# Other distances between the side steps of a Hyena filter, in a layer kernel that runs on one TensorE queue

## The chip, the cores and the metric

The kernel runs on one core of a Trainium2 chip, in one launch. The metric is device time in microseconds (us), the median of several runs. A profile of one execution shows what each engine did: TensorE (PE, with its weight loads as PEld), VectorE (DVE), ScalarE (ACT), GpSimd (POOL) and SyncE (SP). Each engine has one queue and works through it in order.

## The reference

One encoder layer in float32, 512 tokens of width 2048. A Hyena branch and an attention branch read the same normalised input, are gated and merged, and a SwiGLU network follows. The change concerns the Hyena branch, whose long filter comes out of a small network:

```python
def implicit_filter(L, w1, b1, w2, b2, w3, b3, w4, freq):
    ...
    h = jnp.sin(fr * (z @ w1 + b1))
    h = jnp.sin(fr * (h @ w2 + b2))
    h = jnp.sin(fr * (h @ w3 + b3))
    h = h @ w4
    ...
    h_fwd = h[:, :HYENA_W] * decay
    h_bwd = h[:, HYENA_W:] * decay
    k = jnp.concatenate([h_fwd, zeros, h_bwd[:0:-1]], axis=0)
    return k / jnp.sum(jnp.abs(k), axis=0, keepdims=True)

def bidir_fft_conv(u, k):
    uf = jnp.fft.rfft(u, n=2 * L, axis=1)
    kf = jnp.fft.rfft(k, n=2 * L, axis=0)
    return jnp.fft.irfft(uf * kf[None], n=2 * L, axis=1)[:, :L]

def hybrid_layer(...):
    proj = rms_norm(x, mix_norm_g) @ w_in
    u_h, q, k, v, g = jnp.split(proj, [c0, c1, c2, c3], axis=-1)
    x0, x1, hv = jnp.split(centred_short_conv(u_h, hy_conv_w, hy_conv_b), 3, axis=-1)
    z = hv * x1
    y_h = (bidir_fft_conv(z, filt) + hy_bias * z) * x0
    ...
```

## The kernel before

Activations lie transposed: 128 channels on the partitions, 512 tokens along the row. Weights come in 128x128 blocks, eight to a tile (`wr`), through SP's queue. ScalarE rounds a tile to a high part (`wh`), VectorE subtracts to get the low part (`wl`), with three buffers for each (`wblk`, L175). A **product** is the three matmuls (high x high, high x low, low x high) of one weight block with one row block of x (`mm3`, L199).

TensorE's matmuls stand in the order in which the program is written. The main stream is: 64 products for the first four column blocks of `w_in` (x1 and hv of the first two channel blocks, `px`), 16 for each further column (`px`, `phv`; three columns to a channel block, eight channel blocks in four quarters), so 384 products in all; then 64 steps for the keys and values (`kv`, products 384 to 448), then the queries (`q`). Each finished Hyena column gets a short convolution (L576): one multiplication by the row scale `rbc` and two scalar forms on VectorE, one activation on ScalarE. x1 and hv of a channel block give `z`, and `zf`, its two halves.

Between the products stand **side steps**. They are Python generators in one queue. After each product the function `step()` (L144) lowers a counter, and when it is at zero it runs the front generator up to its next `yield n`, which sets the counter to n products. The numbers behind `yield` are therefore distances on TensorE, in products. For each quarter q the side steps are, in order:

- `mlp_gen` (L312, once): the three layers of the filter network (`hp` on TensorE, then seven operations on VectorE and a sine on ScalarE), MLP_WAIT products apart
- `taps_gen`: four pairs of tap matmuls (`fp`), two products apart; VectorE multiplies them with the decay (`fd`, `bd`) and folds them into a sum and a difference (`hs`, `hd`)
- `filter_gen`: transposes of these (`ktp`), a turn and a split on ScalarE and VectorE (`kr`, `k000h`, `k000l` and the like), the halved transform (`kp`), from it the spectra `G` and `K`, which go to DRAM (`kd`, POOL's queue)
- `conv_gen`: transposes of z (`ztp`, split into `zt`), the forward transform (`up`), the product with the filter's spectrum, read back from DRAM (`kc`), on VectorE (`cu`, `cv`, `Y`, split into `Yt`), the taps of the next quarter, and the inverse transform (`ab`), whose result times x0 is `yh`.

PSUM has eight banks for all of this. After the kv chunk, `flush()` runs what is left of the queue, the pool of the Hyena buffers is given up, and the rope table `rpk` is loaded by ScalarE's queue into memory that they held. Keys are normalised and rotated (`vh`, `kscr`, `kqn`, `ko`) and transposed (`kT0p`) 20 products into the queries.

The lines that the change touches: MLP_WAIT (L36), W_FETCH (L55) with the branch of it in `wblk` (L190 to 194), and the distances in `filter_gen` and `conv_gen`.

Of the kernel before, what the change touches and what calls it, by code (L numbers as in the profile page):

```python
# [11 lines left out]
F32 = mybir.dt.float32  # L12
F32R = mybir.dt.float32r
AF = mybir.ActivationFunctionType
ALU = mybir.AluOpType
# [8 lines left out]
NQ = 4  # L24
# [8 lines left out]
HYENA_LAST = 0, 13, 14, 15  # L33
ATT_LAST = 4, 5, 6, 7, 0, 1, 2, 3
G_EARLY = 7
MLP_WAIT = 26  # L36
Z_WAIT0 = 16
N_WARM = 10
XW = 4
# [12 lines left out]
STD_ORDER = (*range(EARLY_ACTS, NSTD), *range(EARLY_ACTS))  # L52
NEARLY = 5
W_FIRST = 16, 72
W_FETCH = ()  # L55

C_X0, C_X1, C_HV, C_Q, C_KV, C_GH, C_GA = 0, 1024, 2048, 3072, 4096, 4608, 6656

# [57 lines left out]
def layer_kernel(tc, wpk, xT, par, flt, zemb, w4, decT, tb2, rope, qkg, out):  # L116
    nc = tc.nc
# [12 lines left out]
    def ps_tile(name):  # L130
        return banks["pool"].tile([P, S], F32, tag="ps", bufs=banks["n"], name=name)
# [4 lines left out]
    def transpose(out, src):  # L136
        tc.keep_in_program_order(nc.tensor.transpose(out, src, ident))
# [31 lines left out]
    def tmp(name):  # L169
        return tpool.tile([P, S], F32, tag="tmp", bufs=5, name=name)  # L170
# [4 lines left out]
    def wblk(nb=1):  # L175
        st = state
        if st["pos"] >= BLK:
            i = st["tile"]
            raw = wpool.tile([P, BLK * P], F32, tag="raw", bufs=2, name=f"wr{i}")
            hi = wpool.tile([P, BLK * P], F32R, tag="whi", bufs=3, name=f"wh{i}")  # L180
            lo = wpool.tile([P, BLK * P], F32R, tag="wlo", bufs=3, name=f"wl{i}")
            st.update(tile=i + 1, pos=0, hi=hi, lo=lo, raw=raw)

        i, n = st["tile"] - 1, {1: XW // 2, 2: XW}.get(st["tile"], BLK)
        if st["pos"] % n == 0:
            c = slice(st["pos"] * P, (st["pos"] + n) * P)
            with tc.high_priority() if W_FIRST[0] <= i < W_FIRST[1] else nullcontext():
                nc.sync.dma_start(st["raw"][:, c], wpk[i, :, c])
                nc.scalar.copy(st["hi"][:, c], st["raw"][:, c])  # L189
                if i in W_FETCH:  # L190
                    nc.scalar.activation(st["lo"][:, c], st["raw"][:, c], AF.Copy, scale=-1.0)
                    nc.gpsimd.dma_start(st["lo"][:, c], wpk[i, :, c], accum_op=ALU.add)
                else:
                    nc.vector.tensor_tensor(st["lo"][:, c], st["raw"][:, c], st["hi"][:, c].bitcast(F32), ALU.subtract)  # L194
        a = st["pos"] * P
        st["pos"] += nb
        return st["hi"][:, a:a + nb * P], st["lo"][:, a:a + nb * P]

    def mm3(ps, ah, al, bh, bl, first, last, **kw):  # L199
        mm(ps, ah, bh, first, False, **kw)  # L200
        mm(ps, ah, bl, False, False, **kw)
        mm(ps, al, bh, False, last, **kw)

    def group(ps, act, k0=0, k1=None):
        n = len(act)
        for k in range(k0, n if k1 is None else k1):
            wh, wl = wblk()
            mm3(ps, wh, wl, act[k][0], act[k][1], k == 0, k == n - 1)
            step()

    def split(pool, src, th, tl, bh, bl, name):
        hi = pool.tile([P, S], F32R, tag=th, bufs=bh, name=name + "h")
        lo = pool.tile([P, S], F32R, tag=tl, bufs=bl, name=name + "l")
        nc.scalar.copy(hi, src)
        nc.vector.tensor_tensor(lo, src, hi.bitcast(F32), ALU.subtract)
        return hi, lo
# [27 lines left out]
    def pcol(name, i=0):  # L244
        a = PC[name] + i
        return prm[:, a:a + 1]
# [45 lines left out]
    def work(name):  # L292
        return cw(name, [P, S], "wk", 7)
# [7 lines left out]
    def part(i, low, a, b):  # L301
        return CS[i][:, low * S + a:low * S + b]
# [9 lines left out]
    def mlp_gen():  # L312


        hcur = zem
        yield MLP_WAIT
        w4_load(0)
        for l in range(3):
# [14 lines left out]
            if l == 2:  # L333
# [4 lines left out]
                mlp["h"] = hh, hl  # L338
            yield MLP_WAIT
            if l == 0:  # L340
# [5 lines left out]
    def w4_load(q):  # L346
        w4t[q] = tmp(f"w4r{q}")
        for h in range(2):
            nc.scalar.dma_start(w4t[q][h * 64:(h + 1) * 64], w4[q])

    def w4_parts(q):

        w4r = w4t[q]
        w4h = tpool.tile([P, S], F32R, tag="tmp", bufs=5, name=f"w4h{q}")
        w4s = cw(f"w4s{q}", [P, 512], "w4s", 1, F32R)
        nc.scalar.copy(w4h[64:], w4r[64:])
        nc.scalar.copy(w4s[:64], w4r[:64])
        nc.vector.tensor_tensor(w4s[64:], w4r[64:], w4h[64:].bitcast(F32), ALU.subtract)
        w4t[q] = w4s
# [40 lines left out]
    def filter_gen(q):  # L400
        rn, hs_l, hd_l = folded.pop(q)
        if q + 1 < NQ:
            w4_load(q + 1)
        taps = []
        for i, src in enumerate((hs_l, hd_l)):
            tps = [ps_tile(f"ktp{q}{i}{j}") for j in range(2)]
            for j, tp in enumerate(tps):
                for n in range(4):
                    o = n // 2 * 256 + j * P
                    transpose(tp[:, n * P:(n + 1) * P], src[n % 2][:, o:o + P])  # L410
            for j in range(2):
                t = tmp(f"kt{q}{i}{j}")
                nc.scalar.activation(t, tps[1 - j], AF.Copy, scale=pcol("sina" if i == j else "nsina"))
                turned = work(f"kr{q}{i}{j}")
                nc.vector.scalar_tensor_tensor(turned, tps[j], pcol("cosa"), t, ALU.mult, ALU.add)
                taps.append(split(cv, turned, "kh", "kl", 4, 4, f"k{i}{q}{j}"))
            yield 3
        if q + 1 < NQ:
            w4_parts(q + 1)
        yield 6  # L420


        kd[q] = dpool.tile([256, 6 * 256], F32, tag=f"kd{q}", bufs=1, name=f"kd{q}")
        spectra = [], []
        for i in range(2):
            g = [ps_tile(f"kp{q}{i}{w}") for w in range(2)]
            for w in range(2):
                mm3(g[w], part(w, 0, 3 * P, 4 * P), part(w, 1, 3 * P, 4 * P), *taps[2 * i + (w ^ i)], True, True)
            cc = tmp(f"kc{q}{i}")
            nc.scalar.copy(cc, g[0])  # L430
            for fb, (a, b, op) in enumerate(((g[1], cc, ALU.add), (cc, g[1], ALU.subtract))):
                spectra[fb].append(work(f"G{q}{fb}{i}"))
                nc.vector.scalar_tensor_tensor(spectra[fb][i], a, pcol("inner"), b, ALU.mult, op)
            yield 3
        for fb in range(2):
            g = spectra[fb]
            sin, nsin = ("sinw", "nsinw")[::1 - 2 * fb]
            cr, ci = tmp(f"kcr{q}{fb}"), tmp(f"kci{q}{fb}")
            nc.scalar.activation(cr, g[0], AF.Copy, scale=pcol("cosw", fb))
            nc.scalar.activation(ci, g[1], AF.Copy, scale=pcol("ncosw" if fb else "cosw"))  # L440
            k1, k2, k3 = (work(f"K{i}{q}{fb}") for i in range(3))
            nc.vector.scalar_tensor_tensor(k1, g[1], pcol(sin, fb), cr, ALU.mult, ALU.add)
            nc.vector.scalar_tensor_tensor(k2, g[0], pcol("nsinw", fb), ci, ALU.mult, ALU.add)
            nc.vector.scalar_tensor_tensor(k3[:, :256], g[1][:, 256:], pcol(nsin, fb), cr[:, 256:], ALU.mult, ALU.add)
            nc.vector.scalar_tensor_tensor(k3[:, 256:], g[0][:, 256:], pcol("sinw", fb), ci[:, 256:], ALU.mult, ALU.add)
            rows = kd[q].rearrange("(p s) c -> p s c", s=2)[:, 1 - fb]
            nc.gpsimd.dma_start(rows[:, :S], k3)
            for i, k in enumerate((k1, k2)):
                nc.gpsimd.dma_start(rows[:, S:].rearrange("p (a b c) -> p a b c", a=2, b=2)[:, :, i],
                                    k.rearrange("p (a c) -> p a c", a=2))  # L450
        filt[q] = rn

    zst, x0st, yh = {}, {}, [None] * HT

    def conv_gen(q):
# [37 lines left out]
                yield 5  # L493
        if q + 1 < NQ:
            yield from taps_gen(q + 1)
        yield 8 if q + 1 < NQ else 14
        abs_ = [work(f"abs{2 * q + c}") for c in range(2)]
        for ph in range(2):
            ab = [ps_tile(f"ab{q}{ph}{c}") for c in range(2)]
# [34 lines left out]
    queue(taps_gen(0))  # L534
    queue(pause(12))
    queue(filter_gen(0))
    w00 = wblk()
    for k in range(KT):
        xr = r3.tile([P, S], F32, tag="r", bufs=16, name=f"xr{k}")
        nc.sync.dma_start(xr, xT[k])  # L540
        hl = r1[k < HT].tile([P, 2 * S], F32R, tag="hl", bufs=HT, name=f"xh{k}")
        hi, lo = hl[:, :S], hl[:, S:]
# [42 lines left out]
    for q in range(NQ):  # L585
        zl, zf_l = [], []
        for c in range(2):
# [19 lines left out]
            zf_l.append(zf)  # L607
        zst[q] = (zl, zf_l, side["n"] + (Z_WAIT0 if q == 0 else 10))
        queue(conv_gen(q))
        if q + 1 < NQ:  # L610
            queue(filter_gen(q + 1))
# [866 lines left out]
```

## Time and profile before

| | us |
|---|---|
| median of 3 runs (2528.24 to 2529.08) | 2528.87 |
| the profiled execution, as a whole | 2527.96 |
| its span in the profile | 2526.2 |
| mean granted TensorE clock in it | 0.999 of full speed |
| end of the last inverse transform of the Hyena branch | 377.2 |

Times in the profile count from the start of the span. A line of a timeline gives start, duration, engine, source line, operation, output and inputs, and in brackets the idle time before it and what ended that. A line of the waits gives the waiting engine and line, whom it waited for, and in us the total, the number of waits and the longest. A line of the windows gives, for a stretch of time, its length and the busy time of each engine with its number of instructions, then the granted clock and the DMA share and rate.

### The profile page before, as it was taken

What the parts mean: (1) busy time and instruction counts of PE and PEld (TensorE: products, weight loads), DVE (VectorE), ACT (ScalarE), POOL (GpSimd) and SP (SyncE); (2) the same over time, 40 slices, a digit from 0 to 9 for tenths busy, and PEclk for the clock granted to TensorE, in tenths of its full rate; (3) what the DMA queues carried; (4) which work ended last, traced back from release to release, by engine and by line L of the source; (5) the groups of instructions that cost most, each with busy time, mean ns of one, the idle gap of its engine ahead of it and who ended that gap; (6) DMA issues with size and microseconds to landing.
All of it is one profiled execution on the core that took longest, in us unless ns stands there. A gap on an engine that the chain in (4) does not pass through costs nothing.

```text
span 2526.2 us, 34432 instructions
## 1 busy us (share of the span) xinstructions
PE 2499.9 (99%) x13114; PEld 2143.5 (85%) x13114; DVE 2089.0 (83%) x2968; ACT 1194.9 (47%) x1779; POOL 182.8 (7%) x295
## 2 busy tenths in 40 slices
PE   9999999999999999999999999999999999999999
PEld 7777778888888888888888888888888888888888
DVE  7889884766479999754899899989998988998888
ACT  6533433655355455443544444444444445445443
POOL 0001112110000000000000000000000002001111
PEclk9999999999999999999999999999999999999999
DMA  6334443222554444544333333333333349557754
GB/s 213 109 116 140 130 131 113 84 80 101 175 175 162 155 139 158 191 164 145 119 112 125 117 120 131 109 134 113 130 121 121 118 137 223 149 146 184 193 156 109
DMA packets 113538, 350.42 MB, mean 139 GB/s; under 512 B 13987, under 2 KB 15267, under 8 KB 113148
## 3 DMA queue, kind: packets, MB, share of 16 engines
q1 hardware_dynamic: 70128, 248.02, 29.6%
q0 software_dynamic: 22832, 63.19, 9.6%
q10 hardware_dynamic: 20412, 37.00, 4.7%
q8 instruction: 103, 1.69, 0.3%
q14 instruction: 63, 0.52, 0.1%
HBM read 297.56 MB, written 54.26 MB: 139 GB/s over the span
## 4 chain that ended last, share of the span: by engine, by line
PE 79%; DVE 1%; ACT 0%; issue 0%; ACTq 0%
PE fx L134 19%; PE fy L134 10%; PE b L134 7%; PE o L134 7%; PE gx L134 6%; PE d L134 5%; PE fz L134 5%; PE dx L134 4%; PE ex L134 3%; PE gy L134 3%; PE ey L134 2%; PE dy L134 2%; PE gz L134 2%; PE q L134 1%; PE dz L134 1%; PE av L134 1%
## 5 line engine op out<-in xcount | busy, mean ns | idle before, releaser
L194 DVE TENSOR_TENSOR wl<-wr,wh 128x1024 fp32r<-128x1024 f32 (+1 forms) x168 | 201.2, 1198 | 123.2 <-ACT wh L189 122.9
L189 ACT CAST wh<-wr 128x1024 fp32r<-128x1024 f32 (+1 forms) x168 | 173.2, 1031 | 274.2 <-PE o L134 66.0
L901 ACT CAST fwhs<-fs 128x1024 fp32r<-128x1024 f32 x176 | 184.9, 1051 | 87.5 <-PE fz L134 69.1
L903 DVE TENSOR_TENSOR fwls<-fs,fwhs 128x1024 fp32r<-128x1024 f32 x176 | 214.3, 1218 | 4.5 <-ACT fwhs L901 4.4
L901 ACT CAST fwha<-fa 128x1024 fp32r<-128x1024 f32 x132 | 139.0, 1054 | 151.1 <-PE fx L134 82.9
L134 PE MATMUL px<-xh,wh 128*128 128x512 f32 x576 | 180.9, 396 | 0.0
L134 PE MATMUL fx<-fX,fwhs 128*128 128x512 f32 x704 | 175.4, 391 | 0.6 <-DVE fv L945 0.6
L134 PE MATMUL fy<-fX,fwhs 128*128 128x512 f32 x704 | 175.5, 391 | 0.0
L134 PE MATMUL fx<-fX,fwha 128*128 128x512 f32 x704 | 172.0, 391 | 0.2 <-DVE c L950 0.2
L903 DVE TENSOR_TENSOR fwla<-fa,fwha 128x1024 fp32r<-128x1024 f32 x132 | 161.3, 1222 | 9.9 <-ACT fwha L901 9.7
L134 PE MATMUL o<-ms,wh 128*128 128x512 f32 x512 | 157.7, 389 | 0.0
L134 PEld LDWEIGHTS fx<-fX,fwhs 128*128 128x128 f32 x704 | 129.3, 188 | 25.7 <-DVE fv L945 0.9
L134 PEld LDWEIGHTS fx<-fX,fwha 128*128 128x128 f32 x704 | 129.3, 188 | 25.4 <-issue 0.6
L134 PEld LDWEIGHTS fy<-fX,fwhs 128*128 128x128 f32 x704 | 129.4, 188 | 24.8
L134 PEld LDWEIGHTS px<-xh,wh 128*128 128x128 f32 x576 | 107.5, 189 | 24.7 <-issue 2.4
L134 PE MATMUL d<-act,wh 128*128 128x512 f32 x384 | 118.3, 390 | 0.0
L134 PE MATMUL px<-xh,wl 128*128 128x512 f32 x288 | 113.1, 393 | 0.0
L134 PEld LDWEIGHTS o<-ms,wh 128*128 128x128 f32 x512 | 96.1, 188 | 19.9
L894 DVE TENSOR_TENSOR fs<-fa,fa 128x1024 f32<-128x1024 f32 x88 | 107.1, 1217 | 1.7 <-PE o L134 1.0
L894 DVE TENSOR_TENSOR fs<-fs,fa 128x1024 f32<-128x1024 f32 x88 | 107.3, 1219 | 1.0 <-PE o L134 0.2
L134 PE MATMUL o<-ms,wl 128*128 128x512 f32 x256 | 99.7, 389 | 0.0
L134 PE MATMUL fy<-fX,fwls 128*128 128x256 f32 x704 | 98.7, 283 | 0.0
(970 smaller groups left out, 5909.0 us busy)
## 6 DMA issues: line engine op xcount, KB each, us to landing
fa<-wpk SPq DMA_DIRECT2D x176, 512.0 KB, 3.9
wr<-wpk SPq DMA_DIRECT2D x162, 512.0 KB, 3.5
ga<-wpk SPq DMA_DIRECT2D x60, 512.0 KB, 3.9
da<-wpk SPq DMA_DIRECT2D x32, 512.0 KB, 3.8
ea<-wpk SPq DMA_DIRECT2D x32, 512.0 KB, 4.2
actd<-c POOLq DMA_DIRECT2D x41, 256.0 KB, 4.3
actr<-actd ACTq DMA_DIRECT2D x41, 256.0 KB, 4.2
x2d<-dt POOLq DMA_DIRECT2D x32, 256.0 KB, 5.4
```

Of the source, the lines that this page charges most:

```text
L134: tc.keep_in_program_order(nc.tensor.matmul(out, lhsT=lhsT, rhs=rhs, start=start, stop=stop, **kw))
L189: nc.scalar.copy(st["hi"][:, c], st["raw"][:, c])
L194: nc.vector.tensor_tensor(st["lo"][:, c], st["raw"][:, c], st["hi"][:, c].bitcast(F32), ALU.subtract)
L894: raws["sum"] = nc.vector.tensor_tensor(t, a, b, ALU.add).ins
L901: nc.scalar.copy(hi, w)
L903: raws["wl"] = nc.vector.tensor_tensor(lo, w, hi.bitcast(F32), ALU.subtract).ins
```

## The change

The layers of the filter network come 20 products apart in place of 26. In each quarter twelve products more are put around side steps: two ahead of the transposes of the filter (`ktp`), three ahead of the halved transform (`kp`), two behind its last part, and three (in the last quarter two) ahead of the inverse transform (`ab`). With what the queue itself takes for a generator's end, the distance from the last `kp` to `ztp` goes from four products to eight. A branch that was never taken is removed.

```diff
-MLP_WAIT = 26
+MLP_WAIT = 20
...
-W_FETCH = ()
...
-                if i in W_FETCH:
-                    nc.scalar.activation(st["lo"][:, c], st["raw"][:, c], AF.Copy, scale=-1.0)
-                    nc.gpsimd.dma_start(st["lo"][:, c], wpk[i, :, c], accum_op=ALU.add)
-                else:
-                    nc.vector.tensor_tensor(st["lo"][:, c], st["raw"][:, c], st["hi"][:, c].bitcast(F32), ALU.subtract)
+                nc.vector.tensor_tensor(st["lo"][:, c], st["raw"][:, c], st["hi"][:, c].bitcast(F32), ALU.subtract)
...
     def filter_gen(q):
         rn, hs_l, hd_l = folded.pop(q)
         if q + 1 < NQ:
             w4_load(q + 1)
+        yield 2
         taps = []
...
         if q + 1 < NQ:
             w4_parts(q + 1)
-        yield 6
-
+        yield 9
...
             for i, k in enumerate((k1, k2)):
                 nc.gpsimd.dma_start(rows[:, S:].rearrange("p (a b c) -> p a b c", a=2, b=2)[:, :, i],
                                     k.rearrange("p (a c) -> p a c", a=2))
+            yield 2
         filt[q] = rn
...
         if q + 1 < NQ:
             yield from taps_gen(q + 1)
-        yield 8 if q + 1 < NQ else 14
+        yield 11 if q + 1 < NQ else 16
```

Counted on TensorE's queue, the steps stand behind these products:

| step | quarter 0 | quarter 1 | quarter 2 | quarter 3 |
|---|---|---|---|---|
| filter network, before | 27, 53, 79 | | | |
| after | 21, 41, 61 | | | |
| first taps, before | 106 | 175 | 248 | 321 |
| after | 82 | 160 | 245 | 330 |
| first `ktp`, before | 128 | 201 | 274 | 347 |
| after | 106 | 191 | 276 | 361 |
| first `kp`, before | 140 | 213 | 286 | 359 |
| after | 121 | 206 | 291 | 376 |
| first `ztp`, before | 147 | 220 | 293 | 366 |
| after | 132 | 217 | 302 | 387 |
| first `up`, before | 155 | 228 | 301 | 374 |
| after | 140 | 225 | 310 | 395 |
| first and second `ab`, before | 191, 195 | 264, 268 | 337, 341 | 408, 412 |
| after | 179, 183 | 264, 268 | 349, 353 | 431, 435 |

Three places show it in the engines' queues. On TensorE, around `rs1bcp` (the matmuls that spread the row scale, behind product 80), there stood before the last layer of the network (`hp`), the matmuls of x0 (`px`) and no taps:

```order
L134 MATMUL hp_623<-h_474,fl 128x512
L134 MATMUL px_543<-xh_516,wh_597 128x512 x2
L134 MATMUL px_543<-xh_516,wl_598 128x512
L134 MATMUL rs1bcp<-rs1dg,rs1ones 128x128 x4
L134 MATMUL px_689<-xh_130,wh_691 128x512 x2
L134 MATMUL px_689<-xh_130,wl_692 128x512
L134 MATMUL px_689<-xh_151,wh_691 128x512 x2
L134 MATMUL px_689<-xh_151,wl_692 128x512
L134 MATMUL px_689<-xh_177,wh_691 128x512 x2
```

Now the first taps (`fp`) follow two products behind it:

```order
L133 MATMUL px_560<-xh_516,wh_614 128x512 x2
L133 MATMUL px_560<-xh_516,wl_615 128x512
L133 MATMUL rs1bcp<-rs1dg,rs1ones 128x128 x4
L133 MATMUL px_689<-xh_130,wh_691 128x512 x2
L133 MATMUL px_689<-xh_130,wl_692 128x512
L133 MATMUL px_689<-xh_151,wh_691 128x512 x2
L133 MATMUL px_689<-xh_151,wl_692 128x512
L133 MATMUL fp_706<-hh,w4s_393 128x512
L133 MATMUL fp_706<-hl,w4s_393 128x512
```

The last layer has moved ahead by 18 products, the first taps by 24.

On VectorE, behind the row scale, the first short convolutions (`x1o`, `hvo`, `yh`) were over before the first taps were multiplied (`fd`, `bd`):

```order
L581 SCALAR_TENSOR_TENSOR hvo_672<-hv1u,prm,hvo_672 128x511
L578 TENSOR_TENSOR x01u<-px_689,rbc 128x512
L600 TENSOR_TENSOR z_678<-hvo_672,x1o_666 128x512
L194 TENSOR_TENSOR wl_866<-wr_864,wh_865 128x1024
L604 TENSOR_TENSOR zf_680<-z_678 128x256 x2
L580 SCALAR_TENSOR_TENSOR yh_750<-x01u,prm,yh_750 128x511
L375 TENSOR_TENSOR fd_801<-fp_803,dec_799 128x512
L581 SCALAR_TENSOR_TENSOR yh_750<-x01u,prm,yh_750 128x511
L375 TENSOR_TENSOR bd_802<-fp_813,dec_799 128x512
```

Now the taps' rows stand among them:

```order
L600 TENSOR_TENSOR zf_663<-z_661 128x256 x2
L370 TENSOR_TENSOR fd_704<-fp_706,dec_702 128x512
L576 SCALAR_TENSOR_TENSOR x1o_666<-x11u,prm,x1o_666 128x511
L576 SCALAR_TENSOR_TENSOR hvo_672<-hv1u,prm,hvo_672 128x511
L577 SCALAR_TENSOR_TENSOR x1o_666<-x11u,prm,x1o_666 128x511
L577 SCALAR_TENSOR_TENSOR hvo_672<-hv1u,prm,hvo_672 128x511
L576 SCALAR_TENSOR_TENSOR yh_683<-x00u,prm,yh_683 128x511
L596 TENSOR_TENSOR z_678<-hvo_672,x1o_666 128x512
L577 SCALAR_TENSOR_TENSOR yh_683<-x00u,prm,yh_683 128x511
L600 TENSOR_TENSOR zf_680<-z_678 128x256 x2
L370 TENSOR_TENSOR bd_705<-fp_716,dec_702 128x512
```

The first `fd` has moved from behind the second z to behind the first.

On ScalarE, at the end of the Hyena branch, the loads of the rope table and of the gains of k and q stood ahead of the last weight tiles before `vh`:

```order
L514 ACTIVATE abl_3389<-ab_3357,rn_2715 128x256
L189 CAST wh_3461<-wr_3460 128x1024
L654 DMA rpk<-rope 128x1024
L655 DMA gaink<-qkg 128x256
L189 CAST wh_3491<-wr_3490 128x1024
L655 DMA gainq<-qkg 128x256
L189 CAST wh_3646<-wr_3645 128x1024
L189 CAST wh_3676<-wr_3675 128x1024
L778 ACTIVATE vh_3530<-kv_3206,rs1ry 128x256
```

Now they stand directly ahead of `vh`, and `gainq` among the squares of k (`kscr`):

```order
L188 CAST wh_3676<-wr_3675 128x1024
L650 DMA rpk<-rope 128x1024
L651 DMA gaink<-qkg 128x256
L774 ACTIVATE vh_3530<-kv_3126,rs1ry 128x256
...
L665 ACTIVATE kscr_3567,kss<-kv_3128 128x128 x2
L651 DMA gainq<-qkg 128x256
L665 ACTIVATE kscr_3571,kss<-kv_3129 128x128 x2
L224 ACTIVATE krt<-kss 128x8
L677 ACTIVATE kqn_3587<-kv_3126,kry 128x128 x2
```

`rpk` has moved behind the weight tile `wh_3676`, three tiles later, and `gainq` behind all four `vh`.

## The prediction

> **What bounds the kernel now.** The page comes first: which engine is busy, and what ends last.
>
> ```profile
> span 2526.2 us, 34432 instructions
> PE 2499.9 (99%) x13114; PEld 2143.5 (85%) x13114; DVE 2089.0 (83%) x2968; ACT 1194.9 (47%) x1779; POOL 182.8 (7%) x295
> ```
>
> TensorE is the bound almost everywhere, so a gain has to be time in which it stood still or ran slowly. The change touches only the first 448 products (a product is the three matmuls of one weight block with one row block of x). So the second view is the windows, cut at the first key transpose (`ktp`) of each Hyena quarter.
>
> ```profile
> core 0: us, PE busy (x) PEld busy (x) DVE busy (x) ACT busy (x) POOL busy (x), PEclk, DMA share, GB/s
> 100.80:170.20 69.40, 65.88 (x308) 54.27 (x307) 59.05 (x89) 27.32 (x42) 7.17 (x12) 0.98 0.40 126
> 170.20:240.30 70.10, 65.80 (x308) 53.18 (x307) 64.11 (x107) 30.22 (x50) 7.21 (x12) 1.00 0.41 132
> 240.30:313.40 73.10, 67.84 (x308) 54.07 (x307) 66.60 (x109) 30.57 (x48) 7.20 (x12) 0.98 0.39 127
> 313.40:377.10 63.70, 57.93 (x277) 47.31 (x276) 57.49 (x88) 26.09 (x41) 7.19 (x12) 1.00 0.41 132
> ```
>
> Three quarters issue the same 308 matmuls and take 69.4, 70.1 and 73.1 us. What they need comes from rows where TensorE runs without a break (the chain of waits later on, and the timeline):
>
> ```profile
> 494.68 0.87 PE pt L137 x8
> 495.55 0.70 PE q L134 x3
> ...
> 165.09 0.33 PE L134 MATMUL ab<-CS,Yt011h 128*128 128x256 f32 x1
> 165.32 0.34 PE L134 MATMUL ab<-CS,Yt011h 128*128 128x256 f32 x1
> ```
>
> A 512-wide matmul costs 0.227 us (0.68 in a product of three), a transpose 0.109, a pair of the inverse transform (256 and 128 wide) 0.23. A quarter has 73 products (219 matmuls), 32 more 512-wide ones (8 taps, 12 `kp`, 12 `up`), 24 transposes and 16 pairs: 251 x 0.227 + 24 x 0.109 + 16 x 0.23 = 63.3 us. The last stretch has 65 products and no taps: 219 x 0.227 + 2.6 + 3.7 = 56.0. So TensorE loses 6.1, 6.8, 9.8 and 7.7, in all **30.4 us**. That is the whole pool. (The idle time that the view gives is smaller, 4.3 of 70.1 us, because the ends of matmuls are modelled.) The waits view shows on whom:
>
> ```profile
> PE ktp L137 <- DVE hs L394: 3.7, 3, 1.9
> PE up L134 <- DVE zt00l L215: 3.2, 1, 3.2
> PE ab L134 <- ACT Yt311h L214: 1.5, 1, 1.5
> PE kp L134 <- DVE k131l L215: 1.2, 1, 1.2
> ```
>
> All are side steps (filter, forward, inverse transform) that come due before VectorE has their input. VectorE is 64.11 of 70.1 and 66.60 of 73.1 us busy: here two engines share the bound. The largest part of its own idle time is one wait, for the filter's round trip through DRAM:
>
> ```profile
> DVE cu L486 <- DMA kc<-kd: 11.8, 4, 4.6
> ```
>
> **The change, part by part.** *The removed fetch branch* costs nothing: its tuple was empty and no instruction came from it. *TensorE's work* is the same; POOL's queue keeps its order, and on SP one x load moves up one place. Everything lies in *when* side steps come due.
>
> *Twelve products more per quarter.* A quarter after the change has 85 products, so TensorE needs 63.3 + 12 x 0.68 = 71.5 us. VectorE's price of those products comes from back-to-back starts:
>
> ```profile
> 236.93 0.41 DVE L394 TENSOR_TENSOR hd<-fd,bd 128x256 f32<-128x256 f32 x1
> 237.25 0.42 DVE L395 TENSOR_TENSOR hd<-fd,bd 128x256 f32<-128x256 f32 x1
> 237.59 0.69 DVE L375 TENSOR_TENSOR fd<-fp,dec 128x512 f32<-128x512 f32 x1
> 238.19 0.68 DVE L375 TENSOR_TENSOR bd<-fp,dec 128x512 f32<-128x512 f32 x1
> 238.79 0.69 DVE L578 TENSOR_TENSOR hv5u<-phv,rbc 128x512 f32<-128x512 f32 x1
> ...
> 242.28 1.22 DVE L194 TENSOR_TENSOR wl<-wr,wh 128x1024 fp32r<-128x1024 f32 x1
> 243.42 0.74 DVE L581 SCALAR_TENSOR_TENSOR hvo<-hv5u,prm,hvo 128x511 f32<-128x511 f32 x1
> 244.08 0.48 DVE L516 SCALAR_TENSOR_TENSOR abs<-ab,rn,abl 128x256 f32<-128x256 f32 x1
> ```
>
> That is 0.33 for a half row, 0.60 for a row, 0.66 for a scalar form, 1.14 for a weight tile. 48 products (three columns) bring 6 weight tiles, three short convolutions (0.60 + 2 x 0.66) and one z with its two halves: 6.84 + 5.76 + 1.26 = 13.9 us, 0.289 a product. Twelve more cost VectorE 3.5 us a quarter, against 8.2 for TensorE: it is given 4.7 us more than it is asked for. Of the twelve, three stand ahead of the inverse transform (`ab`), two between it and `ktp`, three between `ktp` and `kp`, four between `kp` and the transposes of z (`ztp`). So `zt` has 2.7 us more behind `kp`, `kp` 2.0 more behind `ktp`, and `ktp` 3.4 more behind the taps; the longest wait for each was 3.2, 1.2 and 1.9.
>
> Two ends follow. **If TensorE is the bound throughout**, all 30.4 go, but for the first `ktp` below. **If VectorE stays the bound and keeps all its idle time**, the stretches last 3.5 us longer each (the last, with 9 more products, 2.6), but do more. That sum needs the start.
>
> *The filter network earlier.* Its layers stand at products 21, 41 and 61 (before 27, 53, 79), the taps at 82 to 88 (106 to 112), the first `ktp` at 106 (128). The third layer leaves the stretch behind `rs1bcp`, where it ran among the first short convolutions; now these meet the taps. On VectorE the second row of the second `hs` is the input of `ktp`. Ahead of it, from the row scale `rbc` on, the new order has 12 full rows, 10 scalar forms, 10 half rows, 3 weight tiles and 0.8 us of small ones (`rs1bcp` itself keeps its time, since three layers stand ahead of it in both orders):
>
> ```profile
> 65.35 1.05 PE L134 MATMUL rs1bcp<-rs1dg,rs1ones 128*128 128x128 f32 x8
> ...
> 66.16 0.70 PE L134 MATMUL px<-xh,wh 128*128 128x512 f32 x2
> ...
> 66.44 0.59 ACT L275 COPY rbc<-rs1bcp 128x512 f32<-128x512 f32 x1
> 66.44 1.23 DVE L194 TENSOR_TENSOR wl<-wr,wh 128x1024 fp32r<-128x1024 f32 x1
> ```
>
> From 67.6: 7.2 + 6.6 + 3.3 + 3.4 + 0.8 = 21.3, so 88.9. TensorE reaches `ktp` after 26 products and 8 tap matmuls, 66.16 + 17.7 + 1.8 = 85.7, and needs that row half a microsecond later: **a new wait of about 3 us**. It is bounded by 0 and by some 5, since the second decay row takes the buffer of the first and can land late. Behind it on TensorE stand the products, and all of it is paid. The chain then starts at 88.7 in place of 100.8.
>
> Now the sums. TensorE bound: 30.4 - 3.0 = 27.4. VectorE bound: 88.7 + 69.4 + 70.1 + 73.1 + 63.7 + 3 x 3.5 + 2.6 = 378.1 for the end of the last `ab`, 1.0 later than before, but 435 products are done there in place of 412; 23 x 0.68 = 15.7, so 14.7 gained. Idle of 6.0 and 6.5 us a quarter can take some of the 3.5, so the truth lies between; no row is nearer to one end, and I take the middle, **21.0**.
>
> *The clock.* The granted clock dropped twice, behind such waits:
>
> ```profile
> 130.00:134.00 4.00, 4.00 (x12) 3.13 (x12) 0.00 (x0) 0.00 (x0) 1.08 (x2) 0.64 0.55 198
> 256.00:260.00 4.00, 3.87 (x11) 3.12 (x12) 3.44 (x6) 2.96 (x6) 0.00 (x0) 0.60 0.00 0
> ```
>
> Each cost about 1.5 us (4 x 0.36, 4 x 0.40), both inside the 30.4. The second followed single waits of 0.89 us at most:
>
> ```profile
> 253.37 0.49 PE L134 MATMUL kp<-k020h,CS 128*128 128x512 f32 x1 [0.89 <-ACT k020h L214]
> ```
>
> So the remaining waits may cost a drop: between 0 and two; I take 0.9, a little over half of one, and 20.1 is left. The Trainium skill ("TensorE: Matmul & The Clock Gate", section "Why this matters for your kernels") asks only that no idle gap exceeds about 3 us. The first drop, behind 3.2 us, agrees; the second does not, and the measurement decides. By that rule the term would be 0 and the gain 21.0.
>
> *The end of the last quarter* moves from product 412 to 435, close to the end of the kv chunk (448). On ACT's queue the load of the rope table `rpk` waits for the last `yh`; behind it stand the evacuations `vh` and weight casts, and, behind the POOL work on the table, the `gainq` load, now ahead of the last `kscr`:
>
> ```profile
> 376.98 0.23 PE L134 MATMUL ab<-CS,Yt311l 128*128 128x128 f32 x1
> ...
> 381.04 0.33 ACTq L654 DMA_DIRECT2D rpk<-rope  x1
> ...
> 389.62 0.34 ACTq L655 DMA_DIRECT2D gainq<-qkg  x1
> ...
> 399.75 0.47 ACT L778 ACTIVATE vh<-kv,rs1ry 128x256 fp32r<-128x256 f32 x1 [2.35 <-PE kv L134]
> ...
> 404.66 0.28 ACT L669 ACTIVATE kscr<-kv 128x128 f32<-128x128 f32 x1 [0.53 <-DVE vl L779]
> ```
>
> `gainq` comes 12.5 us behind the last `ab`. The kv chunk now ends 13 products, 8.9 us, behind that `ab`, so `gainq` falls 3.6 us behind the first `vh`; the last `kscr` came 4.9 behind it. Cost 0, with 1.3 us of cover; beyond it, each microsecond by which VectorE's tail comes later delays the heads of k, and with them TensorE at `kT0p`.
>
> Sum: 20.1 us. The profiled execution took 2527.96 (span 2526.2 and 1.76 around it); it becomes 2507.9. The median of the runs is 0.9 above it: **2508.8**.
>
> **The rivals.**
>
> *VectorE bound, with all idle time kept* (14.7, less 0.9 for the clock): 2515. For it: 64.11 of 70.1 busy, in order. Against it: 3.0 of the idle time is a DMA wait that any work can fill.
>
> *The DRAM round trip becomes the bound.* From the last K row to the first `cu`, 10.0 us:
>
> ```profile
> 197.64 0.47 DVE L445 SCALAR_TENSOR_TENSOR K<-G,prm,kci 128x256 f32<-128x256 f32 x1
> 208.12 1.22 DVE L486 TENSOR_TENSOR cu<-up,kc 128x1024 f32<-128x1024 f32 x1 [3.06 <-DMA kc<-kd]
> ```
>
> VectorE now fills 7 us of it with `zt`, a weight tile and the next z column. With other spacing that column may come due elsewhere; in the new order of quarter 1 `cu` already stands ahead of z and its halves (1.3 us). If 4 us of fill go in each quarter and the stretch up to the first, 4 x 4 = 16 takes the 14.7, and with the clock's 0.9 it gives about 2531, no change within the bound below. Against it: the products run on during the wait and bring 0.289 us of fill each.
>
> *The last quarter collides with the kv chunk* (the slower case). PSUM has eight banks; kv holds four from product 384 to the end, and the last quarter's `ztp`, `up` and `ab` (387 to 435) must live in four, where before all but `ab` were over. VectorE's run from the first `cu` to the last `Yt` takes 26.6 us:
>
> ```profile
> 349.48 1.23 DVE L486 TENSOR_TENSOR cu<-up,kc 128x1024 f32<-128x1024 f32 x1 [3.06 <-DMA kc<-kd]
> ...
> 375.45 0.68 DVE L215 TENSOR_TENSOR Yt311l<-Y,Yt311h 128x512 fp32r<-128x512 f32 x1
> ```
>
> If TensorE has to stand still for all of it, 20.1 turns into a loss of 6.5: 2535. It decides from a wait of 20 us on. Against it: the second `up` pair needs only the banks of two `ztp`, freed by one copy and one subtraction each, so the wait stays at the `ab`, whose inputs come no sooner anyway.
>
> *That the change does not do what it says* is ruled out by the order: the steps stand at the products named.
>
> **How the numbers follow.** Forecast 2509 (2502 to 2513): 0.64. VectorE bound, 2515 (2513 to 2523): 0.15. Round trip: 0.13. Collision: 0.08. The range 2501 to 2524 has TensorE's end (2528.87 - 27.4 = 2501.5) and the second case in it and leaves the last two out. A run of this kernel can be told from no change from 0.2% on, 5 us. Faster by more: 0.64 + 0.15 = 0.79; within: 0.13; slower: 0.08.
>
> **What would show it.** Right: the three stretches between `ktp` last 71.5 to 74 us with some 344 matmuls each; no wait for `zt`; a wait of some 3 us at the first `ktp`, at 86 us; the kv chunk ends near 380 and everything behind is shifted whole. VectorE bound: stretches over 73.5, waits at `kp` and `ktp` in every quarter. Round trip: `cu` idle over 20 us in all. Wrong altogether: a wait before `ab` of the last quarter or before the first `kT0p`, or a wait of TensorE on weights or x in the first 60 us, where the earlier layers meet the loading of x.

## The result, and the profile after

The changed kernel takes 2512.22 us (median of 6 runs, 2510.36 to 2513.91) where the kernel before takes 2528.55 in the same runs. The ratio is 0.9934, with an interval of 0.9922 to 0.9947: faster by 16 us. The forecast was 2508.8, its range 2501 to 2524. The profiled execution took 2511.97 us, its span 2510.2, so the span is 16.0 us shorter where 20.1 had been forecast.

The head of the page of the changed kernel:

```profile
span 2510.2 us, 34435 instructions
PE 2493.9 (99%) x13114; PEld 2141.5 (85%) x13114; DVE 2087.8 (83%) x2968; ACT 1190.0 (47%) x1777; POOL 183.0 (7%) x295
```

Its windows, cut as the prediction cut them, from the first `ktp` of a quarter to the next, and to the end of the last `ab` (length, busy time of each engine, granted clock, DMA):

```profile
85.92:163.18 77.26, 73.74 (x344) 61.42 (x343) 66.85 (x113) 33.67 (x53) 7.16 (x12) 0.98 0.41 133
163.18:237.38 74.20, 72.80 (x344) 59.90 (x343) 66.56 (x107) 31.16 (x51) 7.20 (x12) 1.00 0.45 139
237.38:312.11 74.73, 73.20 (x344) 59.88 (x343) 69.21 (x110) 32.48 (x52) 7.18 (x12) 1.00 0.41 128
312.11:376.00 63.89, 62.72 (x304) 52.37 (x303) 57.01 (x86) 24.74 (x37) 7.19 (x12) 1.00 0.43 138
```

TensorE needs 71.5 us for each of the first three (85 products) and 56.0 + 9 x 0.68 = 62.1 for the last. It loses 5.8, 2.7, 3.2 and 1.8, in all 13.5 where it lost 30.4: 16.9 came back here, and the span shows 16.0, so 0.9 of it went again outside these stretches, 0.7 of it behind the kv chunk (2125.3 us from there to the end, 2124.6 before).

Of its waits, those that carry what is left (total, number, longest), TensorE's first:

```profile
PE ktp L136 <- DVE hs L389: 4.7, 2, 3.5
...
PE kp L133 <- ACT k111h L209: 0.6, 1, 0.6
...
PE kp L133 <- ACT k021h L209: 0.6, 1, 0.6
```

and VectorE's:

```profile
DVE cu L482 <- DMA kc<-kd: 19.0, 4, 5.9
```

The wait for `zt` is gone, that before `ab` too. A wait at the first `ktp` is new, and VectorE's wait for the filter's round trip has grown from 11.8 us to 19.0. On the timeline of TensorE, the first `ktp`:

```profile
85.92 0.27 PE L136 MATMUL ktp<-ident,hs 128*128 128x128 f32 x1
89.71 1.73 PE L136 MATMUL ktp<-ident,hs 128*128 128x128 f32 x7 [3.52 <-DVE hs L389]
```

and on VectorE's the row for which it waits:

```profile
89.24 0.41 DVE L389 TENSOR_TENSOR hs<-fd,bd 128x256 f32<-128x256 f32 x1
```

TensorE arrives at 85.92 (85.7 forecast), the row starts at 89.24 (it was to be there at 88.9), and the wait is 3.52 us (about 3).

### The profile page after: what moved, and what is told of

Same layout as the page of the kernel before. It is cut to its first block, busy times and chain, and to the rows that moved or that the text cites. A ratio compares the mean times of both kernels' runs of the same rounds, so it can differ in the third digit from the quotient of the medians.

```text
span 2510.2 us, 34435 instructions
## 1 busy us (share of the span) xinstructions
PE 2493.9 (99%) x13114; PEld 2141.5 (85%) x13114; DVE 2087.8 (83%) x2968; ACT 1190.0 (47%) x1777; POOL 183.0 (7%) x295
## 4 chain that ended last, share of the span: by engine, by line
issue 66%; PE 9%; POOL 3%; DVE 2%; DMA 1%; ACT 0%; POOLq 0%; ACTq 0%; DVEq 0%
PE ex L133 3%; PE ey L133 2%; PE q L133 1%; POOL x2d L1288 1%; PE b L133 1%; POOL actd L1263 1%; PE ez L133 1%; POOL bd L1085 1%; PE av L133 0%; DVE eX L860 0%; DMA ea<-wpk 0%; POOL x2d L1208 0%; POOL md L1161 0%; PE sp L133 0%; DVE dt L1346 0%
```

## The experiments

All ratios are to the kernel before in runs on the same chip; the edits are to the changed kernel where nothing else is said. "Lost" is the stretches' length less what TensorE needs in them, worked out as above; where the field is empty it was not worked out. The medians come from different chips, so kernels are compared by their ratios.

| kernel | median, us | ratio | interval | lost by quarter | sum |
|---|---|---|---|---|---|
| before | 2528.55 | 1 | | 6.1, 6.8, 9.8, 7.7 | 30.4 |
| the change | 2512.22 | 0.9934 | 0.9922 to 0.9947 | 5.8, 2.7, 3.2, 1.8 | 13.5 |
| e1_layers20 | 2533.68 | 1.0017 | 1.0009 to 1.0026 | 9.7, 12.1, 10.7, 4.2 | 36.7 |
| e2_layers26 | 2524.04 | 0.9976 | 0.9967 to 0.9986 | | |
| e3_first_ktp_late | 2506.24 | 0.9909 | 0.9894 to 0.9925 | 0.4, 0.4, 4.1, 1.9 | 6.8 |
| e4_less_vector | 2506.12 | 0.9908 | 0.9895 to 0.9922 | 2.5, 1.1, 4.0, 0.8 | 8.4 |
| e5_kp_earlier | 2518.79 | 0.9955 | 0.9941 to 0.9968 | | |
| e6_ab_earlier | 2520.80 | 0.9964 | 0.9951 to 0.9976 | | |
| e7_ztp_earlier | 2523.38 | 0.9968 | 0.9956 to 0.9981 | | |
| e8_ktp_earlier | 2516.29 | 0.9945 | 0.9933 to 0.9958 | | |
| e9_before_no_trip | 2518.95 | 0.9951 | 0.9939 to 0.9964 | 5.4, 4.8, 7.7, 2.9 | 20.8 |
| e10_after_no_trip | 2506.01 | 0.9901 | 0.9887 to 0.9914 | 6.7, 1.3, 0.4, 0.3 | 8.7 |
| e11_up_later | 2503.34 | 0.9890 | 0.9874 to 0.9905 | 0.4, 0.5, 0.7, 3.4 | 5.0 |
| e12_last_kp_later | 2502.80 | 0.9891 | 0.9874 to 0.9907 | | |

**The two halves of the change, each alone.** First the network's layers alone, on the kernel before:

```diff
-MLP_WAIT = 26
+MLP_WAIT = 20
```

> The kernel of before with the layers of the filter network 20 products apart and all other distances as before. Theory A (distances decide: TensorE pays for each side step that comes due before VectorE has its input): the first ktp stands at product 104, so its wait is that of the changed kernel and a product or two longer (4 to 5 us, and some 1.7 us behind it at a lower clock), and the waits of quarters 1 and 2 stay about as in before, since the period of 73 products stays. Only the last quarter has room, since its ztp waits for z anyway. 2528 to 2534 us. Theory B (the early start is what pays, the twelve products more only keep it in step): the chain of the Hyena branch starts 12 us earlier and keeps most of that; 2513 to 2519 us.

It is slower than before, by 4.3 us. Its windows, cut in the same way:

```profile
84.70:157.70 73.00, 66.72 (x308) 55.34 (x307) 62.73 (x103) 29.99 (x49) 7.17 (x12) 0.95 0.42 136
157.70:233.10 75.40, 68.01 (x309) 54.19 (x307) 66.28 (x109) 30.79 (x48) 7.20 (x12) 0.98 0.38 123
233.10:307.10 74.00, 68.43 (x308) 55.72 (x307) 65.55 (x109) 31.93 (x53) 7.17 (x12) 0.95 0.39 125
```

and its largest wait:

```profile
PE ktp L137 <- DVE hs L394: 9.1, 4, 5.4
```

The early start pays nothing by itself (theory B falls): it adds the wait at the first `ktp`, 5.4 us here. The rest is more telling. These quarters hold 73 products (308 matmuls) and last 73.0 to 75.4 us, as long as the changed kernel's with 85 products (344). The comparison is not clean, since the first of them holds the new wait and the clock was lower in all three (0.95, 0.98, 0.95). Beside the kernel before, whose quarters of 73 products last 69.4, 70.1 and 73.1, the changed kernel's are longer by 4.3 (without the first wait), 4.1 and 1.6 us, where the twelve products are 8.2 us of work for TensorE. About half of that work or more fills time in which TensorE stood or ran slowly.

Then the distances alone: the changed kernel with `MLP_WAIT = 26`.

> The changed kernel with the layers of the filter network 26 products apart again, so that every side step behind them comes 24 products later; the last inverse transforms fall behind the kv chunk (product 448). Theory A: no wait at the first ktp (4.7 us and the 1.7 us at a lower clock behind it are saved), waits in the quarters as in the changed kernel, but a wait of 5 to 15 us before the last ab, since VectorE needs some 27 us from the first cu to the last Yt and 20 us are left, and the heads of k behind it come late. 2513 to 2524 us. Theory B: with the late start the gain is lost as a whole, 2525 us or more. If there is no wait at the end, 2506 to 2508.

2524.0, the very end of theory A's range and one us from theory B's, so two thirds of the gain are lost. The waits show how: `ktp` waits 0.5 us in all for `hs`, as A has it, but the last `ab` pair falls behind the kv chunk, where nothing covers it. (In the quarters three waits of 2.3, 1.3 and 0.9 us are there that the changed kernel does not have, the first of them at `ktp` for a short convolution, `x07u`.) On TensorE's timeline:

```profile
381.56 0.38 PE L133 MATMUL ab<-CS,Yt310h 128*128 128x256 f32 x1 [1.21 <-ACT Yt310h L209]
383.77 0.33 PE L133 MATMUL ab<-CS,Yt310l 128*128 128x128 f32 x1 [1.83 <-DVE Yt310l L210]
387.61 0.58 PE L133 MATMUL ab<-CS,Yt311h 128*128 128x256 f32 x1 [1.21 <-ACT Yt311h L209]
388.70 0.48 PE L133 MATMUL ab<-CS,Yt311l 128*128 128x128 f32 x1 [0.51 <-DVE Yt311l L210]
408.65 0.30 PE L136 MATMUL kT0p<-ident,ko 128*128 128x128 f32 x1 [1.66 <-issue]
409.88 0.33 PE L136 MATMUL kT0p<-ident,ko 128*128 128x128 f32 x1 [0.93 <-DVE ko L688]
```

That is 4.8 us at `ab` and, with two more of 0.67 and 0.41, 3.7 at `kT0p`, where the heads of k come late. Behind the first two of these waits the granted clock was also lower, 0.51:

```profile
384.60:395.00 10.40, 8.69 (x29) 7.19 (x29) 9.32 (x21) 3.41 (x9) 0.00 (x0) 0.51 0.30 95
```

At full clock the 8.69 us of work would have taken 4.3 less. So the wider spacing needs the earlier start to end ahead of the kv chunk's end: the two halves belong together.

**The new wait.** Six products more ahead of the first `ktp`:

```diff
-        yield 2
+        yield 2 if q else 8
```

> The changed kernel with six products more ahead of the first ktp (quarter 0 alone), so that all behind it comes six products later (last ab at 441 in place of 435). Theory A: the wait at the first ktp (3.7 us) and the stretch at a lower clock behind it (1.7 us) go, nothing takes their place: 2506 to 2508 us. Rival: VectorE has a backlog there, and the wait comes back at the first kp or at ztp: 2510 to 2512. Second rival: the last quarter now ends too close to the heads of k, and a wait before kT0p takes 3 us or more of it.

2506.24, as theory A has it. The first three windows:

```profile
90.20:162.10 71.90, 71.90 (x344) 60.04 (x343) 66.67 (x109) 32.52 (x50) 7.16 (x12) 1.00 0.45 143
162.10:234.00 71.90, 71.90 (x344) 60.05 (x343) 67.78 (x110) 32.50 (x51) 7.20 (x12) 1.00 0.47 143
234.00:309.60 75.60, 73.99 (x345) 61.37 (x344) 66.71 (x109) 32.07 (x50) 7.18 (x12) 0.98 0.40 126
```

Two quarters run without a wait, at 71.9 us for the 71.5 that were worked out. The kp waits of quarters 1 and 2 went with it, which I had not expected: all side steps stand six products further on among the columns, and the order on VectorE around `kp` is another. A wait of 1.6 us before `ab` of quarter 2 is new.

**What VectorE's work is worth.**

```diff
         nc.scalar.activation(o, u, AF.Identity, ...)
+        if name.startswith("x0"):
+            return o
```

> The changed kernel without the two scalar forms of the short convolution of x0 (its outer two taps are left out), 16 instructions of 0.66 us less on VectorE, 2.6 us in each quarter. Theory A (what is left of the loss is VectorE's backlog between the filter's round trip and kp): the waits at kp and ktp of quarters 1 to 3 and the slow stretches by them, 1.6, 3.4 and 1.7 us, go for the most part, and the wait at the first ktp is 1.3 us shorter: 5 to 8 us less, 2504 to 2507. Rival (they are latencies of ScalarE, DMA or the order of the queue): only the 1.3 us, 2510 to 2512.

This kernel leaves out the outer two taps of the short convolution of x0, so its output is another; VectorE has 16 scalar forms less. 2506.12: 5.1 of the 13.5 us lost came back. But the theory holds only in part. Quarter 1 lost 1.6 less and quarter 3 1.0 less, the first `ktp` waited 1.91 us and the clock did not drop behind it; quarter 2 lost 4.0, more than before the edit. There `kp` waits (1.2 and 1.1) for a chain of `kr`, `k021h` and `k121l` that is queued behind weight tiles on both engines. VectorE is busy for 12.39 of the 13.00 us from 243 to 256, so the order in its queue and a lack of its time can't be told apart there.

**Each distance taken back.** Four kernels, each with one of the edits undone (`yield 9` to 6 ahead of `kp`; 11 and 16 to 8 and 14 ahead of `ab`; no `yield 2` in the loop at the end, which runs twice, so four products; no `yield 2` at the start):

> The changed kernel with the three products ahead of kp taken back (six in place of nine behind the transposes), so a period of 82. Local theory (each step has its own deadline, and what counts is how many products stand ahead of it): kp is the step that still waits in quarters 1 and 2, so this undo costs most of the four, some 2 us in each of these and up to 1 in the others: 2516 to 2519 us. Period theory (VectorE is the bound over a whole quarter, and only the number of products in a quarter counts, 0.68 - 0.29 = 0.39 us for each and each of four quarters): 3 x 4 x 0.39 = 4.7 us, 2517, with the waits spread over ktp, kp, ztp and ab.

> The changed kernel with the products ahead of ab taken back (8 and 14 in place of 11 and 16), period 82. Local theory: the changed kernel has no wait before ab, and 2 us less leave at most a short one in a quarter; ktp comes three products earlier too, with the taps as far ahead of it as before, so 0 to 3 us: 2512 to 2515. Period theory: 4.7 us, 2517, with waits at ktp and kp of quarters 1 to 3.

> The changed kernel with the four products between kp and ztp taken back (two behind each half of the last part), period 81. Local theory: the wait for zt of quarter 0 (3.2 us in before) comes back in part, and cu's wait for the filter's round trip hides it elsewhere: 1 to 4 us, 2513 to 2516. Period theory: 4 x 4 x 0.39 = 6.3 us, 2518.5, spread over the quarters.

> The changed kernel with the two products ahead of ktp taken back, period 83. Local theory: the first ktp waits 1.4 us longer (its input comes when it came), that of quarter 3 1.4 us longer, the others 0 to 1: 3 to 5 us, 2515 to 2517. Period theory: 2 x 4 x 0.39 = 3.1 us and the 1.4 of the first ktp, 2516.7. (The two hardly differ here; the places of the waits tell them apart.)

By the ratios they cost 5.3, 7.6, 8.6 and 2.8 us (the period theory had 4.7, 4.7, 6.3 and 3.1; the interval of each ratio is some 3 us to each side, and a cost is the difference of two). The local theory gives too little at `ab` and `ztp`, for which it had 0 to 3 and 1 to 4, though beyond the noise by little. In the kernel with the earlier `ab` the waits stand all over the quarter:

```profile
PE ab L133 <- DVE cv L483: 4.3, 1, 4.3
PE ktp L136 <- DVE hs L389: 3.9, 1, 3.9
PE kp L133 <- ACT k121h L209: 1.4, 1, 1.4
PE ab L133 <- DVE bd L370: 1.4, 1, 1.4
```

So none of the four distances is free, and a product is worth 0.35 to 0.69 us in a quarter, whichever step it is put in front of; finer differences these runs can't tell. I read this as a ring: the steps feed each other through VectorE's queue, and a quarter with too few products mostly waits somewhere. The ring's length is no constant, though. With the earlier `ktp`, quarter 1 ran 83 products without a wait, in 70.5 us:

```profile
162.90:233.44 70.54, 70.54 (x338) 58.92 (x337) 63.80 (x99) 30.03 (x45) 7.21 (x12) 1.00 0.43 135
```

**What sets the ring's length.** In quarters 1 and 2 VectorE is busy for 66.56 and 69.21 us of the 74.20 and 74.73; the largest single part of the rest is one gap. Its timeline in the changed kernel, at the first `cu` of quarter 1:

```profile
190.79 0.48 DVE L440 SCALAR_TENSOR_TENSOR K<-G,prm,kci 128x256 f32<-128x256 f32 x1
...
195.70 0.75 DVE L577 SCALAR_TENSOR_TENSOR hvo<-hv4u,prm,hvo 128x511 f32<-128x511 f32 x1
201.73 1.23 DVE L482 TENSOR_TENSOR cu<-up,kc 128x1024 f32<-128x1024 f32 x1 [5.28 <-DMA kc<-kd]
202.88 0.68 DVE L596 TENSOR_TENSOR z<-hvo,x1o 128x512 f32<-128x512 f32 x1
```

`cu` comes 10.5 us after the end of the last K (10.0 in the place that the prediction showed), as the spectrum goes to DRAM and back. `z`, whose inputs `hvo` and `x1o` were there by 196.5, stands behind `cu` in the queue and waits with it. To test whether this gap sets the length, the read was pointed at what quarter 0 had stored. Quarters 1 to 3 then use quarter 0's filter; only the time of these kernels means something:

```diff
-nc.gpsimd.dma_start(kc[ph][p0:p0 + n], kd[q][r0:r0 + n, ph * S:ph * S + 2 * S])
+nc.gpsimd.dma_start(kc[ph][p0:p0 + n], kd[0][r0:r0 + n, ph * S:ph * S + 2 * S])
```

> The kernel of before, in which quarters 1 to 3 read back the filter spectrum that quarter 0 stored, so that the load of kc need not wait for this quarter's store to land (its own way of some 4.6 us stays; the output is that of other filters). Hole theory (the length of a quarter is VectorE's work plus the idle time that cu's wait for the round trip leaves in its queue): cu comes 3 to 5 us earlier in each of three quarters, and these get shorter by 2 to 4 us each, 6 to 12 in all: 2517 to 2524 us beside a kernel before of 2529 to 2530. Rival (that idle time is slack; what makes a quarter long are the local deadlines): within 3 us of before.

> The changed kernel with the same edit. TensorE loses 2.7, 3.2 and 1.7 us in quarters 1 to 3, so no more than 7.6 can go. Hole theory: 4 to 7 of them go, 2505 to 2508 us. Rival (slack): 2510 to 2513.

Both came out as the gap has it. `cu`'s wait in the first and in the second kernel:

```profile
DVE cu L486 <- DMA kc<-kd: 4.4, 1, 4.4
```

```profile
DVE cu L482 <- DMA kc<-kd: 3.4, 1, 3.4
```

Only quarter 0 still waits. The kernel before loses 9.6 us less in its quarters (its ratio is 0.9951, 12 us), the changed one 4.8 less. Quarters 1 to 3 of the latter then lose 2.0 in all, in place of 7.6, although quarter 0, which still makes the round trip and has the wait at the first `ktp`, lost 6.7. In the kernel before 20.8 of the 30.4 us stay without the trip, so there it is a third of the loss; in quarters 1 to 3 of the changed kernel it is most of what is left.

The same gap can be filled without another result. Beside the later first `ktp`, the forward transform moves four products down:

```diff
-            yield 2 + 4 * i
+            yield 2 + 8 * i
...
-        yield 11 if q + 1 < NQ else 16
+        yield 7 if q + 1 < NQ else 12
```

> The kernel with the first ktp six products later, and in every quarter the forward transform (up) four products later and the distance ahead of ab four shorter, so that ktp, kp, ztp and ab stay where they are. VectorE's queue then has 6.8, 6.7, 2.9 and 2.3 us of work between the last K and the first cu in place of 5.5, 5.5, 2.3 and 2.3 (from durations of the profiles). Hole theory: the filled idle time, some 3 us, comes off the waits that are left (ab and kp of quarters 2 and 3, 5.9 us): 1 to 3 us less than the 2506.2 of that kernel, 2503 to 2505. Rival: the taps, which come four products later too, are late for ktp, and cu is late for ab: 2507 to 2512.

2503.34, 0.9890 of before, the lower part of the forecast. Its first three windows:

```profile
90.10:162.00 71.90, 71.90 (x344) 60.05 (x343) 68.01 (x109) 33.43 (x51) 7.16 (x12) 1.00 0.45 143
162.00:234.00 72.00, 72.00 (x345) 60.06 (x344) 68.16 (x112) 31.59 (x49) 7.20 (x12) 1.00 0.44 143
234.00:306.20 72.20, 72.20 (x345) 60.15 (x344) 64.32 (x106) 31.35 (x48) 7.19 (x12) 1.00 0.41 132
```

and `cu`'s wait:

```profile
DVE cu L482 <- DMA kc<-kd: 9.6, 3, 4.9
```

`cu`'s wait falls from 16.1 us in the kernel with only the later `ktp` to 9.6, and TensorE is the bound in three quarters. The gain over that kernel is 4.8 us by the ratios, within their intervals, and 1.7 by the spans of the two profiles, where quarter 2 loses 3.4 less and quarter 3 1.5 more. What is clearer is that both are faster than the change: no run of either takes over 2506.93 us, and none of the change less than 2510.36.

Last, in this kernel's last quarter, `kp` three products later and `ab` where it was:

```diff
-        yield 9
+        yield 9 if q + 1 < NQ else 12
...
-        yield 7 if q + 1 < NQ else 12
+        yield 7 if q + 1 < NQ else 9
```

> The kernel with up four products later, and in the last quarter kp, ztp and up three products later still (the distance ahead of ab three shorter, so ab stays). There kp waited 2.2 us for VectorE, and that is what is left of the loss. Local theory: the three products fill that wait and K comes no later, so 1 to 2 us less: 2501.5 to 2502.5 beside 2503.3 (that kernel on another chip; as a ratio to before, 0.9885 beside 0.9890). Rival: VectorE's work up to the last Yt ends when it ended (369.4 us), TensorE reaches ab two us earlier, and the wait moves there whole: no change, 2503 to 2504.

2502.80 at 0.9891 beside 0.9890: no difference that these runs can tell. In the profile `kp` waits 0.5 us in the last quarter in place of 1.8, 0.6 comes back at `ab`, and the stretch lasts 65.0 us in place of 65.5. So part of the wait moved, as the rival has it, but the runs don't decide between the two.

## Why the prediction was right, and where it was off

**The pool** (30.4 us of TensorE standing or running slowly between the first `ktp` and the last `ab`) was the right place: 16.9 came back there, and nowhere else.

**The new wait** was right in place, cause and time: 3.5 us in place of 3.0. Experiment e3 takes it away, and with it waits at `kp` that it was not aimed at.

**The clock** cost 1.7 us in place of 0.9. Behind the new wait the granted clock was 0.56:

```profile
85.92:91.10 5.18, 1.66 (x10) 1.39 (x8) 4.82 (x16) 3.60 (x7) 0.00 (x0) 0.87 0.63 209
91.10:93.50 2.40, 2.40 (x8) 1.96 (x7) 1.49 (x2) 1.20 (x2) 0.00 (x0) 0.56 0.39 152
```

(5.18 x 0.13 + 2.40 x 0.44 = 1.7.) The two drops of before are gone.

**The middle between the two bounds** is the term that was off. The prediction put the truth halfway between TensorE as the bound and VectorE with all its idle time kept, since "Idle of 6.0 and 6.5 us a quarter can take some of the 3.5". It took nothing: the idle time in the same two quarters is 7.6 and 5.5 us (74.20 - 66.56, 74.73 - 69.21). The term was to leave 6.4 us lost, and 8.3 are (13.5 less 3.5 and 1.7). With the 0.5 of the wait, the 0.8 of the clock and the 0.9 behind the kv chunk this makes the 4.1 us between 20.1 and 16.0.

Why the idle time could take nothing is the point that the prediction had and priced as a rival: it is the DRAM round trip, and in a queue that runs in order work can fill it only if it stands ahead of `cu`. The case against that rival, that products run on and bring fill, did not hold in quarter 1, where `z` stood behind `cu`; nor can "any work" fill that wait, as the case against VectorE as the bound had it. But the rival's own price was too high: its 16 us were to turn the gain into nothing, and `cu`'s wait grew by 7.2.

VectorE's bound was the better guess, and its gain had been put too low. It began at 88.7, behind the new wait, but that wait is TensorE's: VectorE is busy for 4.82 of the 5.18 us from 85.92 to 91.10 (the first of the two rows above). Counted from TensorE's arrival, the same sum (the four stretches of before, 276.3, and 3 x 3.5 + 2.6 = 13.1 of work more) ends at 85.7 + 276.3 + 13.1 = 375.1, a gain of 17.7; measured are 376.0 and 16.9. Over the four stretches VectorE's busy time grew by 12.4 us, where the sum had 13.1, and its idle time by 1.4. This fits as a sum only and was worked out afterwards: by quarter the busy time grew by 7.8, 2.5, 2.6 and -0.5, where 3.5, 3.5, 3.5 and 2.6 were put.

The middle of 21.0 had no row behind it. That the time still lies within the main case of 2502 to 2513, 0.8 us from its end, is in part luck: two terms were off in opposite directions, idle time that was not filled and a wait that was counted on VectorE's time too.

**The signs** that were named: 344 matmuls in a stretch and no wait for `zt`, as said. The stretches were to last 71.5 to 74 us; less the first wait they last 73.7, 74.2 and 74.7, the last two past the upper end and all three past the 73.5 named for VectorE. The waits at `kp` and `ktp` in every quarter that belonged to that sign did not come: `kp` waits in quarters 1 and 2 alone, `ktp` in quarters 0 and 3. `cu`'s idle time is 19.0, just under the 20 named for the round trip. The kv chunk ends at 384.9 us, not near 380, mostly by the gain that is missing. One wait of TensorE on x in the first 60 us, named as a sign of being wrong altogether, is there: 0.67 us ahead of the first product, on a rounded tile (`xh`). It cost next to nothing: that product starts at 5.84 in place of 5.69 us, and `rs1bcp` at 65.41 in place of 65.35.

**The end of the last quarter.** No wait at `ab` or `kT0p`, as said, with 13 products between the last `ab` and the end of the kv chunk. `gainq` was issued 5.4 us behind the first `vh` (383.04 and 388.43; 3.6 forecast), past the cover of 1.3, and cost nothing that the trace shows. What the collision costs, once `ab` falls behind the chunk, e2 shows: 8.4 us of waits and 4.3 of lower clock. That is the place of the rival, at half of its 26.6.

**Open.** The first two quarters of e1 are 3.6 and 5.3 us longer than in before, with the same distances; only their place among the columns differs. In the first, the wait of 5.4 us and the clock of 0.95 behind it account for that. In the second `kp` and `ab` wait; which rows of VectorE make that was not tried. The 0.7 us behind the kv chunk was not traced to a place. That VectorE's queue behind `cu` holds back the quarters 1 to 3 of the changed kernel is shown by e10 (2.0 us lost in place of 7.6); that a quarter as a whole behaves as a ring of fixed length is an argument, which the 70.5 us above speaks against.

## What to carry to other kernels

When two engines share a bound, ask of the idle time of the second one what ends it: here time that an in-order queue spent behind a DMA wait was not free for more work, except where that work was put ahead of the waiting instruction. Distances between steps that feed each other can act as a ring; look for what sets its length, then give the other engine as much work per turn as fits in it. And an earlier start that nothing else needs is a cost, to be paid only as far as a wider spacing has to end in time.

## What the hardware showed unasked

The length of a wait alone did not decide whether the granted clock dropped. In the kernel with the earlier `ztp`, on TensorE's timeline and in the window behind it:

```profile
89.63 0.98 PE L136 MATMUL ktp<-ident,hs 128*128 128x128 f32 x7 [3.65 <-DVE hs L389]
```

```profile
88.00:95.00 7.00, 5.37 (x31) 4.66 (x32) 5.52 (x14) 4.35 (x8) 0.00 (x0) 1.00 0.43 141
```

and in the one with the later first `ktp`:

```profile
295.27 0.35 PE L133 MATMUL ab<-CS,Yt200h 128*128 128x256 f32 x1 [1.13 <-DVE cu L482]
296.40 0.35 PE L133 MATMUL ab<-CS,Yt200h 128*128 128x256 f32 x1 [0.48 <-DVE cv L483]
```

```profile
297.00:300.00 3.00, 3.00 (x13) 2.71 (x13) 3.00 (x5) 0.00 (x0) 0.00 (x0) 0.52 0.14 41
```

3.65 us of standing left the clock at 1.00; 1.13 and 0.48 us brought it to 0.52 for three. Where it dropped, it cost 1.4 us or more in the places looked at (3.00 x 0.48 here, 1.7 at the first `ktp` of the changed kernel, 4.3 in e2), on top of the wait. What decides it these runs do not show. The limit of about 3 us for one idle gap, which the prediction quoted from the Trainium skill ("TensorE: Matmul & The Clock Gate", section "Why this matters for your kernels"), agrees with the wait of 3.52 us above and with neither of these two.
